# Where the down projection keeps its weight sums and its operand slots, and when its last stores are issued

## Chip, cores and metric

One NeuronCore of a Trainium2 chip runs the kernel. The metric is the device time of one execution in microseconds (us). Five engines work side by side, each on its own list of instructions in order: TensorE (PE, matrix products), VectorE (DVE), ScalarE (ACT), GpSimd (POOL) and SyncE (SP), whose list here holds the DMA issues. An engine that waits for a semaphore holds up everything behind it on its own list.

## What is computed

The model has two layers. Each is a mixer, then a feed-forward part (FFN), then a gated residual (PLE). The change lies in the second product of the FFN, `w_down`, and touches the seam to the PLE behind it:

```python
def swiglu(h, w_gate, w_up, w_down):
    return (jax.nn.silu(h @ w_gate) * (h @ w_up)) @ w_down
...
        h = h + swiglu(rmsnorm(h, norm_ffn_g[i]), ffn_w_gate[i], ffn_w_up[i], ffn_w_down[i])
        e = rmsnorm(p[i] @ ple_w_proj[i], ple_post_norm_g[i])
        h = h + e * jax.nn.sigmoid(rmsnorm(h, ple_norm_g[i]) @ ple_w_gate[i])
```

There are 1024 rows, 1024 columns in the model and 2816 in the FFN, all in fp32. A product of fp32 operands is made of three products of halves: each operand is split into a high half (a cast on ScalarE, line 108) and a low half (operand minus high half, on VectorE, line 109), and high by high, high by low and low by high are added up.

## The kernel before, in words

Gate/up and down both use a Winograd form of the 2 x 2 block product: seven block products instead of eight, each of sums of blocks. `wino` makes four such sums of four blocks, in four operations of 128 x 512. On GpSimd it makes the sums `S` of gate/up's weights (in a pool of two buffers), the sums `Sg` of each of the 11 pairs of gated activations `g`, and the sums `T_dn` of each of the 11 raw weights `wr_dn` of down.

Gate/up (`ffn_gu`) goes over the pairs j = 0 to 10, two groups (gate, up) for each. The products of a group are called by their operand: B11, T1, T2, B21 (bank pgc), T3, B22 (bank pgb, operand tiles HB22h and HB22l), T4. Lines 867, 869 and 871 add the banks into `g` or `u`; lines 935 to 937 multiply u into g. Seven blocks of each pair (three of g, four of Sg) are stored to DRAM in `gfD` (lines 940 to 942).

Down (`ffn_down`) reads these back. It works in four units of pairs: (0, 1), (2, 3, 4), (5, 6, 7), (8, 9, 10). A unit has seven steps, one for each block product. "Step 1.0" below is step 0 of unit 1. Step (gi, wi) uses the stored block gi and the weight block wi, where wi 0 to 3 are blocks of the raw weight and 4 to 7 are the sums T_dn. A step needs a slot of four parts: x (block as stored, later its low half), y (its high half), wh and wl (halves of the weight block). Its work is: a get of x on SP (line 1011), y on ScalarE (line 1016), x minus y on VectorE (line 1017), wh and wl of each pair of the unit (lines 108, 109), then on TensorE 4 x 3 x m matmuls for m pairs (line 1027; 24 in unit 0, 36 in the others), and an evacuation of four banks into `h` (a copy on ScalarE, or an addition on VectorE, line 1030). TensorE alternates two sets of four banks, pda and pdb. In unit 0 the four pdb banks of step 1 are banks that gate/up used.

Memory is divided by pools that are opened in an order written by hand, so that each tile comes to lie on memory that an earlier stage has done with. The kernel's framework makes the instruction wait that first writes there. The slots of down are one large tile `sl12` (six parts of 8 KB for each partition), the pools s0 and s7, `s3` and, once, the two buffers `hn`. T_dn_0 and T_dn_1 (pool `tc_`, two buffers) lie behind `sl12`, on the memory of HB22h and HB22l. The order of instructions on each engine comes from a scheduler that follows the program text and priorities; `self.after([...])` tells it not to place what is inside ahead of the named instruction. Unit 0's preparation is held that way behind `last_sum`, the last line 869.

`ple` follows. It splits the weights of its gate (wr_pg to wh_pg and wl_pg, lines 1118 and 1119, the latter on GpSimd), and norms the rows of h (ss_p on GpSimd, hn_p on VectorE line 203, transposes on line 193). Its first splits and norms are placed among the last steps of down.

Of the kernel before, what the change touches and what calls it, by code (L numbers as in the profile page):

```python
# [9 lines left out]
F32 = mybir.dt.float32  # L10
# [53 lines left out]
class _K:  # L64
# [712 lines left out]
    def wino(self, eng, dst, b, role):  # L777


        sub = lambda o, x, y: eng.tensor_tensor(o, x, y, op=ALU.subtract)  # L780
        if role == "left":
# [3 lines left out]
            sub(dst[3], b[1], dst[1])  # L785
        else:
# [3 lines left out]
            sub(dst[3], b[2], dst[1])  # L790

    def ffn(self, l):
# [3 lines left out]
        with ExitStack() as es:  # L796
# [21 lines left out]
            self.ffn_gu(sp, fp, {"Ta": ta_, "Tb": tb_}, l, H, gD, right)  # L818
# [3 lines left out]
        with ExitStack() as es:  # L822
            self.ffn_down(es, l, gD)
# [3 lines left out]
    def ffn_gu(self, sp, fp, tp_, l, H, gD, right):  # L827
# [98 lines left out]
        for j in range(NFF // 2):  # L926
# [12 lines left out]
            self.wino(gp, [S[:, i] for i in range(4)], [g[:, 0, 0], g[:, 1, 0], g[:, 0, 1], g[:, 1, 1]], "left")  # L939
            nc.sync.dma_start(gD[j, :, 0:2, :], g[:, :, 0, :])  # L940
            nc.sync.dma_start(gD[j, :, 2, :], g[:, 1, 1, :])
            nc.sync.dma_start(gD[j, :, 3:7, :], S)

    def ffn_down(self, es, l, gD):
# [9 lines left out]
        s12 = mk(3).tile([P, 6 * 2048], F32R, name=f"sl12_{l}")  # L954
        self.pad(es, 1, f"ffp2{l}")
        tc_ = mk(6)
        s7 = mk(7)
        self.pad(es, 2, f"ffp3{l}")
        s3 = mk(8)

        slots = itertools.chain((s0, 0, 2, None, 4, s0, 0), (s7, 3, s0, 0) * 3 + (s7, 3), (s0, 0, 3, s0, 0, 3, 0))
# [6 lines left out]
        units = ((0, 1), (2, 3, 4), (5, 6, 7), (8, 9, 10))  # L968
        seen = set()
# [10 lines left out]
        for ui, pairs in enumerate(units):  # L980
            m = len(pairs)
            ws = []
            for p in pairs:
# [4 lines left out]
                self.wino(gp, [T[:, i] for i in range(4)], [q[:, i] for i in range(4)], "right")  # L988
# [5 lines left out]
            for si, (gi, wi, chain, first, (hr, hc)) in enumerate(steps):  # L994
# [4 lines left out]
                slot = next(slots)  # L999
                if slot is None:  # L1000
                    x, y = [self.np.tile([P, D], F32R, tag="hn", bufs=2, name=f"sl{f}{nm}").rearrange("p (j n) -> p j n", j=2) for f in "xy"]
                    slot = s3.tile([P, 2, 2, 512], F32R, name=f"slw{nm}")
                    wh, wl = slot[:, 0], slot[:, 1]
                else:
                    if isinstance(slot, int):
                        slot = s12[:, slot * 2048:][:, :m * 2048]
                    else:
                        slot = slot.tile([P, 6144], F32R, tag="slot", bufs=1, name=f"sl{nm}")[:, :m * 2048]
                    slot = slot.rearrange("p (i j n) -> p i j n", i=4, j=m)
                    x, y, wh, wl = [slot[:, i] for i in range(4)]  # L1010
# [751 lines left out]
```

## Time and profile before

| what | us |
|---|---|
| time before, median of 3 runs | 2976.1 (2974.38 to 2976.13) |
| the profiled execution, its own time | 2976.15 |
| span of the profile of that execution | 2974.3 |
| TensorE busy | 2867.7 (96% of the span) |
| VectorE busy | 1867.2 (63%) |
| GpSimd busy | 1060.5 (36%) |
| granted TensorE clock, mean | 0.985 of full |
| down, layer 0 (first to last matmul) | 1130.5 to 1353.8 |
| down, layer 1 | 2650.0 to 2872.5 |

The profile is of one execution, and its times are counted from the start of the span. The time of an execution is 1.85 us longer than the span. A busy share is an average over stages; how a stage is bound is read from that stage's own rows: what TensorE waited for there, and what the engines that it waited for were doing.

### The profile page before, as it was taken

The numbers are of one execution on the slowest core, as the hardware profiler recorded it, in microseconds if no ns is written. First come the engines' busy times: TensorE is split into PE (matmuls) and PEld (weight loads), VectorE is DVE, ScalarE is ACT, GpSimd is POOL, SyncE is SP. The second block draws the span as 40 slices with busy tenths as digits, with TensorE's granted clock in tenths as the row PEclk, the third lists the DMA queues.
The fourth block names the chain that finished last, engine by engine and source line by source line (L and its number), as shares of the span: only waits on it lengthen the run. The fifth ranks groups of instructions, "written<-read, shape, count | busy, mean of one in ns | idle before, by whom it ended". The sixth has DMA issues, their size and how long they took to land.

```text
span 2974.3 us, 47842 instructions
## 1 busy us (share of the span) xinstructions
PE 2867.7 (96%) x19211; PEld 2388.5 (80%) x19211; DVE 1867.2 (63%) x3274; ACT 1259.4 (42%) x2226; POOL 1060.5 (36%) x931
## 2 busy tenths in 40 slices
PE   7999998999999998999999999999999999999999
PEld 6989876797888886888887777788678888878887
DVE  5799995455444448885466767664445444479871
ACT  4467725544333335434445455443233333344341
POOL 1341000114544436435212443342144455556333
PEclk9999998999999999999999999999999999999999
DMA  4122165201322225534332232223711322245422
GB/s 146 50 51 93 57 191 201 90 30 38 112 106 95 103 107 216 190 108 139 107 127 97 94 111 97 87 94 110 266 64 71 113 102 95 105 172 206 162 87 92
DMA packets 119822, 340.80 MB, mean 115 GB/s; under 512 B 11696, under 2 KB 34608, under 8 KB 101936
## 3 DMA queue, kind: packets, MB, share of 16 engines
q1 hardware_dynamic: 119600, 337.74, 32.9%
q8 instruction: 151, 2.47, 0.3%
q14 instruction: 71, 0.58, 0.1%
HBM read 240.64 MB, written 97.06 MB: 114 GB/s over the span
## 4 chain that ended last, share of the span: by engine, by line
PE 83%; DVE 8%; DMA 3%; ACT 3%; issue 2%; POOL 1%; SPq 0%; DVEq 0%; ACTq 0%; POOLq 0%
PE pga L852 16%; PE pgb L852 8%; PE pso L1369 7%; PE pdb L1027 6%; PE pda L1027 6%; PE psp L1138 6%; PE psz L216 4%; PE pgc L852 4%; PE pskqv L227 3%; PE psow L237 3%; PE psz L1629 2%; PE y L743 2%; PE pswob L237 2%; DVE sc L467 1%; PE tpp L734 1%
## 5 line engine op out<-in xcount | busy, mean ns | idle before, releaser
L1027 PE MATMUL pda<-sl 128*128 128x512 f32 x912 | 217.5, 396 | 12.4 <-DVE sl L109 12.3
L1027 PEld LDWEIGHTS pda<-sl 128*128 128x128 f32 x912 | 173.9, 191 | 51.7 <-DVE sl L109 15.4
L1027 PE MATMUL pdb<-sl 128*128 128x512 f32 x888 | 207.9, 391 | 5.4 <-DVE g L937 3.7
L782 POOL TENSOR_TENSOR S<-wr_gu 128x512 f32<-128x512 f32 x44 | 68.8, 1563 | 395.9 <-DMA wr_gu<-in_w_gu_dram 373.8
L1027 PEld LDWEIGHTS pdb<-sl 128*128 128x128 f32 x888 | 167.1, 189 | 41.9 <-DVE g L937 4.1
L109 DVE TENSOR_TENSOR w2l_gu<-S,w2h_gu 128x1024 fp32r<-128x1024 f32 x44 | 67.2, 1528 | 164.4 <-ACT w2h_gu L108 164.3
L1369 PE MATMUL pso<-hh,wl_od 128*128 128x512 f32 x384 | 157.3, 410 | 0.0
L1369 PE MATMUL pso<-hh,wh_od 128*128 128x512 f32 x384 | 156.9, 409 | 0.0
L1369 PE MATMUL pso<-hl,wh_od 128*128 128x512 f32 x384 | 156.4, 407 | 0.0
L1016 ACT CAST sl<-sl 128x1536 fp32r<-128x1536 f32 (+1 forms) x54 | 74.8, 1386 | 145.8 <-DMA sl<-gfD 143.1
L108 ACT CAST w2h_gu<-S 128x1024 fp32r<-128x1024 f32 x44 | 46.3, 1052 | 186.1 <-PE pga L852 94.1
L1387 DVE SCALAR_TENSOR_TENSOR c<-pso,odcw,c 128x509 f32<-128x509 f32 (+1 forms) x144 | 107.0, 743 | 26.5 <-ACT c L1384 24.9
L1017 DVE TENSOR_TENSOR sl<-sl 128x1536 fp32r<-128x1536 f32 (+1 forms) x54 | 103.3, 1914 | 24.7 <-ACT sl L1016 24.5
L227 PE MATMUL pskqv<-wh_kqv,hh 128*128 128x256 f32 x384 | 109.4, 285 | 0.3 <-ACT wh_kqv L108 0.3
L227 PE MATMUL pskqv<-wh_kqv,hl 128*128 128x256 f32 x384 | 108.7, 283 | 0.0
L227 PE MATMUL pskqv<-wl_kqv,hh 128*128 128x256 f32 x384 | 108.3, 283 | 0.0
L603 DVE TENSOR_SCALAR_CACHE_REDUCE tk_junk<-sc,tk_f 128x1024 int8<-128x1024 f32 (+5 forms) x111 | 102.5, 924 | 1.8
L153 POOL TENSOR_SCALAR nss_f<-nss_f 128x1 f32<-128x1 f32 x16 | 3.2, 200 | 273.2 <-ACT junk_f L152 273.2
L1138 PE MATMUL psp<-wh_pg,hh_p 128*128 128x512 f32 x256 | 100.5, 393 | 0.0
L1138 PE MATMUL psp<-wh_pg,hl_p 128*128 128x512 f32 x256 | 99.7, 390 | 0.0
L1138 PE MATMUL psp<-wl_pg,hh_p 128*128 128x512 f32 x256 | 99.7, 389 | 0.0
L600 ACT ACTIVATE tk_junka<-sc,tk_f 128x512 int8<-128x512 f32 (+2 forms) x93 | 83.7, 900 | 34.5 <-DVE tk_f L618 30.3
(543 smaller groups left out, 9013.3 us busy)
## 6 DMA issues: line engine op xcount, KB each, us to landing
wr_gu<-in_w_gu_dram SPq DMA_DIRECT2D x44, 1024.0 KB
sl<-gfD SPq DMA_DIRECT2D x42, 768.0 KB
gfD<-Sg SPq DMA_DIRECT2D x22, 1024.0 KB
wr_dn<-in_w_dn_dram SPq DMA_DIRECT2D x22, 1024.0 KB
wr_od<-in_w_qkv_dram SPq DMA_DIRECT2D x12, 1024.0 KB
cD<-c SPq DMA_DIRECT2D x24, 512.0 KB
gfD<-g SPq DMA_DIRECT2D x22, 512.0 KB
wr_z<-in_w_z_dram SPq DMA_DIRECT2D x10, 1024.0 KB
```

The costliest lines, as they stand in the source:

```text
L216: nc.tensor.matmul(ps[:M, f * 512:(f + 1) * 512], a[:, kc, c], b[f][:, kc, :], start=(kc == 0 and i == 0), stop=(kc == KC - 1 and i == 2))
L227: nc.tensor.matmul(out, a[:, kc, c], b[:, kc, :], start=(kc == 0 and i == 0), stop=(kc == KC - 1 and i == 2))
L237: nc.tensor.matmul(ps[:, f * 512:(f + 1) * 512], a[:, kc, tsl], b[:, f * 512:(f + 1) * 512], start=(kc == 0 and i == 0), stop=(kc == nk - ...
L600: nc.scalar.activation(jk[:, :n], sc[b], AF.Sign, bias=fb, scale=-1.0, accum_out=c)
L603: v.tensor_scalar(jk[:, :n], sc[b], fb, 0.0, op0=op, op1=ALU.add, accum_out=c)
L852: nc.tensor.matmul(bank, a[:, kc, :], b[:, kc, :], start=first and kc == 0 and m == 0, stop=kc == 3 and m == 2, skip_group_check=True)
L1016: nc.scalar.copy(y, x.bitcast(F32))
L1017: v.tensor_tensor(x, x.bitcast(F32), y.bitcast(F32), op=ALU.subtract)
L1027: nc.tensor.matmul(ps, a[:, i, c], b[:, i, :], start=first and i == 0 and k == 0, stop=i == m - 1 and k == 2, skip_group_check=True)
L1138: nc.tensor.matmul(ps, a[:, kc, c], b, start=kc == 0 and i == 0, stop=kc == KC - 1 and i == 2)
L1369: nc.tensor.matmul(ps[:, f * 512:(f + 1) * 512], a[:, kc, :], b[f][:, kc, :], start=(kc == 0 and i == 0), stop=(kc == KC - 1 and i == 2))
L1387: nc.vector.scalar_tensor_tensor(c[:, e:(f + 1) * 512], ps[:, e - d:(f + 1) * 512 - d], cw[:, k:k + 1], c[:, e:(f + 1) * 512], op0=ALU.mul ...
```

## The change

The down stage is re-divided. The four points that touch the order of work are these.

- `sl12` is replaced by `sa` (32 KB), `sb` (16 KB) and a smaller `s3`. The pool of T_dn_0 and T_dn_1 now comes right behind `sa`, which is the memory of gate/up's weight sums S_20 and S_21; `sb` now lies on HB22h and HB22l.
- `slots` is written anew. Unit 0: n0, a, the middle of `sa`, own (the `hn` buffers and `s3`), sb, n0, a. Units 1 and 2 go round c, n7, n0, a, where c is made of parts of `sb`, `sa` and `s3`. Unit 3: n0, a, c, n0, a, n0, a. A slot is thus used again three steps on at step 1.0, and two steps on at steps 3.5 and 3.6.
- The last pair's three stores are issued behind the get of step 0.6. The sums of unit 1's weights are placed behind the Sg sums of the last pair.
- A step's preparation from unit 1 on is placed behind the preparation of the step before and the evacuation of the third step before.

In `ple` the pool w0 is split in two, so that the first high half lies elsewhere than the other three.

```diff
@@ wino
-        sub = lambda o, x, y: eng.tensor_tensor(o, x, y, op=ALU.subtract)
+        sub = lambda o, x, y: eng.tensor_tensor(o, x, y, op=ALU.subtract).ins
...
-            sub(dst[3], b[1], dst[1])
+            return sub(dst[3], b[1], dst[1])
...
@@ ffn_gu
-            self.wino(gp, [S[:, i] for i in range(4)], [g[:, 0, 0], g[:, 1, 0], g[:, 0, 1], g[:, 1, 1]], "left")
-            nc.sync.dma_start(gD[j, :, 0:2, :], g[:, :, 0, :])
-            nc.sync.dma_start(gD[j, :, 2, :], g[:, 1, 1, :])
-            nc.sync.dma_start(gD[j, :, 3:7, :], S)
+            self.last_Sg = self.wino(gp, [S[:, i] for i in range(4)], [g[:, 0, 0], g[:, 1, 0], g[:, 0, 1], g[:, 1, 1]], "left")
+
+            def store(j=j, g=g, S=S):
+                nc.sync.dma_start(gD[j, :, 0:2, :], g[:, :, 0, :])
+                nc.sync.dma_start(gD[j, :, 2, :], g[:, 1, 1, :])
+                nc.sync.dma_start(gD[j, :, 3:7, :], S)
+
+            if j < NFF // 2 - 1:
+                store()
+        return store
@@ ffn_down
-        s12 = mk(3).tile([P, 6 * 2048], F32R, name=f"sl12_{l}")
+        piece = lambda i, kb: mk(i).tile([P, kb * 256], F32R, name=f"sl{i}_{l}")
+        sa = piece(3, 32)
         self.pad(es, 1, f"ffp2{l}")
         tc_ = mk(6)
+        sb = piece(4, 16)
         s7 = mk(7)
         self.pad(es, 2, f"ffp3{l}")
-        s3 = mk(8)
-
-        slots = itertools.chain((s0, 0, 2, None, 4, s0, 0), (s7, 3, s0, 0) * 3 + (s7, 3), (s0, 0, 3, s0, 0, 3, 0))
+        s3 = piece(8, 8)
+
+        cut = lambda *at: lambda n, nm: [t[:, a if b is None else b * n:][:, :n] for t, a, b in at]
+        run = lambda t, a=0: lambda n, nm: [t[:, a + i * n:a + (i + 1) * n] for i in range(4)]
+        new = lambda p: lambda n, nm: run(p.tile([P, 6144], F32R, tag="slot", bufs=1, name=f"sl{nm}"))(n, nm)
+
+        def own(n, nm):
+            return [self.np.tile([P, D], F32R, tag="hn", bufs=2, name=f"sl{f}{nm}") for f in "xy"] + [s3[:, :n], s3[:, n:2 * n]]
+
+        n0, n7, a, c = new(s0), new(s7), run(sa), cut((sb, 0, 0), (sb, 0, 1), (sa, 6144, None), (s3, 0, 0))
+        slots = itertools.chain((n0, a, run(sa, 4096), own, run(sb), n0, a), (c, n7, n0, a) * 3 + (c, n7), (n0, a, c, n0, a, n0, a))
...
-                self.wino(gp, [T[:, i] for i in range(4)], [q[:, i] for i in range(4)], "right")
+                with self.after([self.last_Sg] if ui == 1 else None):
+                    self.wino(gp, [T[:, i] for i in range(4)], [q[:, i] for i in range(4)], "right")
...
-                nc.sync.dma_start(x.bitcast(F32), gD[pairs[0]:pairs[-1] + 1, :, gi, :].rearrange("j p n -> p j n"))
+                x, y, wh, wl = [t.rearrange("p (j n) -> p j n", j=m) for t in next(slots)(m * 512, nm)]
+                get = nc.sync.dma_start(x.bitcast(F32), gD[pairs[0]:pairs[-1] + 1, :, gi, :].rearrange("j p n -> p j n")).ins
+                if (ui, si) == (0, 6):
+                    with self.after([get]):
+                        store()
...
-                with self.after([self.last_sum] if ui == 0 and si else None):
+                with self.after(prep + evac[:1] if ui else [self.last_sum] if si else None):
                     nc.scalar.copy(y, x.bitcast(F32))
                     v.tensor_tensor(x, x.bitcast(F32), y.bitcast(F32), op=ALU.subtract)
                     for i in range(m):
-                        self.split(wh[:, i], wl[:, i], ws[i][wi])
+                        prep = list(self.split(wh[:, i], wl[:, i], ws[i][wi]))
...
+                evac = evac[-2:] + [out.ins]
@@ ple
-            self.pad(es, 17, f"plp0{l}")
-            w0 = mk("w0")
+            self.pad(es, 1, f"plp0{l}")
+            w0 = [mk("w0a")]
+            self.pad(es, 16, f"plp1{l}")
+            w0 += [mk("w0b")] * 3
...
-                    wt = [(w1[kh] if u else w0).tile([P, 4, 512], F32R, name=f"w{f}_pg{l}_{u}{kh}") for f in "hl"]
+                    wt = [(w1[kh] if u else w0[2 * kh + i]).tile([P, 4, 512], F32R, name=f"w{f}_pg{l}_{u}{kh}") for i, f in enumerate("hl")]
```

The lists of instructions show what this does to the order. TensorE's order in down is the same. On GpSimd, layer 0, behind the Sg sums of pair 9, there stood before:

```order
L780 TENSOR_TENSOR T_dn0_0_9476<-wr_dn0_0_9472 128x512 x2
L780 TENSOR_TENSOR T_dn0_1_9481<-wr_dn0_1_9474 128x512 x2
L780 TENSOR_TENSOR T_dn0_0_9476<-wr_dn0_0_9472,T_dn0_0_9476 128x512
L780 TENSOR_TENSOR T_dn0_1_9481<-wr_dn0_1_9474,T_dn0_1_9481 128x512
L780 TENSOR_TENSOR T_dn0_0_9476<-wr_dn0_0_9472,T_dn0_0_9476 128x512
L780 TENSOR_TENSOR T_dn0_2_9750<-wr_dn0_2_9604 128x512 x2
L780 TENSOR_TENSOR T_dn0_1_9481<-wr_dn0_1_9474,T_dn0_1_9481 128x512
L780 TENSOR_TENSOR T_dn0_2_9750<-wr_dn0_2_9604,T_dn0_2_9750 128x512
L780 TENSOR_TENSOR T_dn0_3_9755<-wr_dn0_3_9606 128x512 x2
L782 TENSOR_TENSOR Sg0_10_9409<-g0_10_9177 128x512
L780 TENSOR_TENSOR Sg0_10_9409<-g0_10_9177 128x512
```

and now there stands, up to the first sums of unit 1:

```order
L780 TENSOR_TENSOR T_dn0_0_9478<-wr_dn0_0_9474 128x512 x2
L780 TENSOR_TENSOR T_dn0_0_9478<-wr_dn0_0_9474,T_dn0_0_9478 128x512 x2
L780 TENSOR_TENSOR T_dn0_1_9483<-wr_dn0_1_9476 128x512 x2
L780 TENSOR_TENSOR T_dn0_1_9483<-wr_dn0_1_9476,T_dn0_1_9483 128x512 x2
L782 TENSOR_TENSOR Sg0_10_9409<-g0_10_9177 128x512
L780 TENSOR_TENSOR Sg0_10_9409<-g0_10_9177 128x512
L780 TENSOR_TENSOR Sg0_10_9409<-Sg0_10_9409,g0_10_9177 128x512
L780 TENSOR_TENSOR Sg0_10_9409<-g0_10_9177,Sg0_10_9409 128x512
L780 TENSOR_TENSOR T_dn0_2_9754<-wr_dn0_2_9605 128x512 x2
L780 TENSOR_TENSOR T_dn0_3_9759<-wr_dn0_3_9607 128x512 x2
```

The eight sums of each kind are no longer mixed: first T_dn0_0, then T_dn0_1, then the Sg sums of the last pair, then the sums of unit 1's weights.

On VectorE, layer 1, from the last line 869 on (sl1_0_0 is the slot of step 0, slx and slw or sl8 belong to step 3, the remaining sl are the slots of steps 1, 2 and 4; lines 1017 and 1027 are the same operation before and after), before:

```order
L869 TENSOR_TENSOR u1_10_24401<-pga1_21_24421,u1_10_24401 128x512
L109 TENSOR_TENSOR sl12_1_24562<-wr_dn1_0_24580,sl12_1_24562 128x512
L1017 TENSOR_TENSOR slx1_0_3_24708<-slx1_0_3_24708,sly1_0_3_24709 128x1024
L1017 TENSOR_TENSOR sl12_1_24562<-sl12_1_24562 128x1024
L936 TENSOR_TENSOR g1_10_24285<-u1_10_24401,g1_10_24285 128x512
L871 TENSOR_TENSOR u1_10_24401<-pgb1_21_24422,u1_10_24401 128x512
L109 TENSOR_TENSOR sl1_0_0_24598<-wr_dn1_1_24582,sl1_0_0_24598 128x512
L109 TENSOR_TENSOR sl12_1_24562<-wr_dn1_1_24582,sl12_1_24562 128x512
L109 TENSOR_TENSOR slw1_0_3_24710<-T_dn1_0_24584,slw1_0_3_24710 128x512
L937 TENSOR_TENSOR g1_10_24285<-pga1_21_24421,g1_10_24285 128x512
```

and now:

```order
L869 TENSOR_TENSOR u1_10_24416<-pga1_21_24436,u1_10_24416 128x512
L109 TENSOR_TENSOR sl3_1_24574<-wr_dn1_0_24597,sl3_1_24574 128x512
L1027 TENSOR_TENSOR slx1_0_3_24725<-slx1_0_3_24725,sly1_0_3_24726 128x1024
L109 TENSOR_TENSOR sl8_1_24596<-T_dn1_0_24601,sl8_1_24596 128x512
L1027 TENSOR_TENSOR sl3_1_24574<-sl3_1_24574 128x1024
L936 TENSOR_TENSOR g1_10_24300<-u1_10_24416,g1_10_24300 128x512
L109 TENSOR_TENSOR sl3_1_24574<-T_dn1_0_24601,sl3_1_24574 128x512
L871 TENSOR_TENSOR u1_10_24416<-pgb1_21_24437,u1_10_24416 128x512
L109 TENSOR_TENSOR sl4_1_24585<-T_dn1_0_24601,sl4_1_24585 128x512
L109 TENSOR_TENSOR sl1_0_0_24615<-wr_dn1_1_24599,sl1_0_0_24615 128x512
L109 TENSOR_TENSOR sl3_1_24574<-wr_dn1_1_24599,sl3_1_24574 128x512
```

The low half that step 0 still lacks, sl1_0_0 from wr_dn1_1, came right behind line 871, and now comes behind three low halves of T_dn1_0 more, one of them ahead of line 936 and one on either side of line 871.

On SP, layer 0, from the last pair's first store (line 941, 940 and 942 before; 942, 943 and 944 after) to the gets of unit 1 (lines 1011 and 1018 are the same operation), before:

```order
L941 DMA gfD0_6508<-g0_10_9177 128x512
L940 DMA gfD0_6508<-g0_10_9177 128x2x512
L1011 DMA sl0_0_5_9679<-gfD0_6508 128x2x512
L976 DMA wr_dn0_5_9926<-in_w_dn0_dram 128x2048
L976 DMA wr_dn0_6_9928<-in_w_dn0_dram 128x2048
L1011 DMA sl12_0_9454<-gfD0_6508 128x2x512
L942 DMA gfD0_6508<-Sg0_10_9409 128x2048
L1011 DMA sl12_0_9454<-gfD0_6508 128x3x512
L1011 DMA sl0_1_0_9765<-gfD0_6508 128x3x512
```

and now, from the get of step 0.5 on:

```order
L1018 DMA sl0_0_5_9680<-gfD0_6508 128x2x512
L993 DMA wr_dn0_5_9930<-in_w_dn0_dram 128x2048
L993 DMA wr_dn0_6_9932<-in_w_dn0_dram 128x2048
L1018 DMA sl3_0_9451<-gfD0_6508 128x2x512
L942 DMA gfD0_6508<-g0_10_9177 128x2x512
L943 DMA gfD0_6508<-g0_10_9177 128x512
L944 DMA gfD0_6508<-Sg0_10_9409 128x2048
L1048 DMA hres0_0_9926<-hB_67 128x1024
L1018 DMA sl0_1_1_9822<-gfD0_6508 128x3x512
L1048 DMA hres0_1_10037<-hB_67 128x1024
L1018 DMA sl4_0_9462<-gfD0_6508 128x3x512
```

The stores of g moved behind the get of step 0.6, the get of step 1.1 (sl0_1_1) follows the store of Sg and one hres, and the get of step 1.0 (sl4, three blocks) comes last.

## Rows read from the trace of the kernel before

**Rows 1.** The page: the span, and the costliest group (busy, mean ns, idle before).

```profile
span 2974.3 us, 47842 instructions
...
L1027 PE MATMUL pda<-sl 128*128 128x512 f32 x912 | 217.5, 396 | 12.4 <-DVE sl L109 12.3
```

**Rows 2.** Timeline, TensorE, layer 0 (start, us, engine line op, out<-in, count [idle<-releaser]).

```profile
1127.64 0.50 PE L852 MATMUL pga<-HT4h,w2h_gu 128*128 128x512 f32 x1 [0.32 <-DVE u L869]
...
1130.50 5.63 PE L1027 MATMUL pda<-sl 128*128 128x512 f32 x24
...
1143.89 2.93 PE L1027 MATMUL pdb<-sl 128*128 128x512 f32 x6 [3.68 <-DVE g L937]
...
1152.18 7.54 PE L1027 MATMUL pda<-sl 128*128 128x512 f32 x23 [4.94 <-DVE sl L109]
...
1176.07 5.60 PE L1027 MATMUL pda<-sl 128*128 128x512 f32 x24
1181.51 8.32 PE L1027 MATMUL pdb<-sl 128*128 128x512 f32 x36
```

**Rows 3.** Timeline, TensorE, the first unit of layer 1.

```profile
2650.03 1.09 PE L1027 MATMUL pda<-sl 128*128 128x512 f32 x4
2652.19 4.81 PE L1027 MATMUL pda<-sl 128*128 128x512 f32 x20 [1.06 <-DVE sl L109]
...
2669.00 8.53 PE L1027 MATMUL pda<-sl 128*128 128x512 f32 x23 [6.33 <-DVE sl L109]
...
2699.95 8.59 PE L1027 MATMUL pdb<-sl 128*128 128x512 f32 x36 [0.48 <-DVE h L1030]
```

**Rows 4.** Windows, layer 0: us; busy of PE, PEld, DVE, ACT, POOL; clock; DMA.

```profile
1130.50:1181.50 51.00, 42.34 (x169) 33.35 (x168) 47.54 (x39) 23.80 (x39) 48.00 (x26) 0.87 0.60 218
1181.50:1353.80 172.30, 171.67 (x758) 141.82 (x757) 145.62 (x164) 66.63 (x85) 69.53 (x38) 1.00 0.43 150
```

**Rows 5.** Timeline, GpSimd, both layers, around the first sums of down.

```profile
1097.30 1.30 POOL L780 TENSOR_TENSOR Sg<-g,Sg 128x512 f32<-128x512 f32 x1 [0.45 <-DVE g L937]
1127.40 6.92 POOL L780 TENSOR_TENSOR T_dn<-wr_dn 128x512 f32<-128x512 f32 x4 [28.80 <-PE pgb L852]
...
2647.51 7.47 POOL L780 TENSOR_TENSOR T_dn<-wr_dn 128x512 f32<-128x512 f32 x4 [26.01 <-PE pgb L852]
```

**Rows 6.** Timeline, VectorE, layer 0, around the end of gate/up.

```profile
1123.85 0.69 DVE L109 TENSOR_TENSOR sl<-wr_dn,sl 128x512 fp32r<-128x512 f32 x1 [1.29 <-ACT sl L108]
1125.63 1.23 DVE L1017 TENSOR_TENSOR sl<-sl 128x1024 fp32r<-128x1024 f32 x1 [1.09 <-ACT sl L1016]
...
1127.50 3.44 DVE L109 TENSOR_TENSOR sl<-wr_dn,sl 128x512 fp32r<-128x512 f32 x2
1130.86 2.31 DVE L1017 TENSOR_TENSOR slx<-slx,sly 128x1024 fp32r<-128x1024 f32 x1
...
1143.15 0.68 DVE L937 TENSOR_TENSOR g<-pga,g 128x512 f32<-128x512 f32 x1
```

**Rows 7.** Timeline, VectorE and ScalarE, layer 1, around the end of gate/up.

```profile
2645.17 0.69 DVE L869 TENSOR_TENSOR u<-pga,u 128x512 f32<-128x512 f32 x1 [2.42 <-PE pga L852]
...
2648.37 1.14 ACT L108 CAST sl<-wr_dn 128x512 fp32r<-128x512 f32 x2 [1.58 <-DMA wr_dn<-in_w_dn_dram]
```

**Rows 8.** Timeline, VectorE, ScalarE and TensorE, steps 3.3 to 3.6 of layer 0.

```profile
1326.21 1.76 DVE L1017 TENSOR_TENSOR sl<-sl 128x1536 fp32r<-128x1536 f32 x1 [1.01 <-ACT sl L1016]
...
1336.55 8.32 PE L1027 MATMUL pda<-sl 128*128 128x512 f32 x36
...
1342.16 1.46 ACT L1016 CAST sl<-sl 128x1536 fp32r<-128x1536 f32 x1
...
1343.66 3.59 DVE L1017 TENSOR_TENSOR sl<-sl 128x1536 fp32r<-128x1536 f32 x1
...
1347.31 6.64 PE L1027 MATMUL pdb<-sl 128*128 128x512 f32 x28 [0.63 <-DVE sl L1017]
```

**Rows 9.** Timeline, SyncE's queue, layer 0, behind the last Sg store.

```profile
1164.52 4.89 SPq L1011 DMA_DIRECT2D sl<-gfD  x2
```

## What I predict, and how

> **What bounds the kernel now.** I read the page first: TensorE is the engine that ends the program, and among its costliest groups only the product of the down stage (line 1027) shows idle time ahead of it worth naming, most of it released by VectorE's low halves on line 109 [rows 1]. The change touches only this stage and its two seams, so I next read TensorE's rows in order of time there. In layer 0 the first unit of down (7 steps of 24 matmuls) runs from 1130.50 to 1181.51, 51.0 us [rows 2]. A step at full speed is 5.44 us (1176.07 to 1181.51), or 0.2267 a matmul, so the unit could take 38.1: 12.9 us are lost. Of these 3.68 are a wait for line 937 in step 1 and 4.94 a wait for line 109 in step 2; most of the rest is slow matmuls behind the waits: 23 of them take 7.54 us from 1152.18 instead of 22 x 0.2267 and 0.39 for the last, 5.38, so 2.16 more. In layer 1 the unit takes 2650.03 to 2699.95, 49.9 us [rows 3]: 11.8 lost, with waits of 1.06, 6.33 and 0.48, and 3.15 of slow matmuls behind the 6.33. The granted clock falls to 0.87 in layer 0's first unit and is 1.00 in the three units behind it, where TensorE is busy 171.67 of 172.30 us [rows 4]. So some 24.7 us in all lie in two places, and each other unit runs at the bound.
>
> Why VectorE is late there: GpSimd stands still for 28.80 and 26.01 us, then starts the sums of the first unit's weights when the last pgb product of gate/up has been issued [rows 5], because these sums were placed in the memory of an operand of that product. From then on both engines are busy for nearly the whole unit, 47.54 and 48.00 of 51.0 us [rows 4], and every VectorE operation with two inputs in SBUF is slower: a low half of 512 columns takes 0.69 alone and 1.72 beside GpSimd (3.44 for two), the 1024-column difference 1.23 and 2.31 [rows 6]. GpSimd's own operation takes 1.30 alone and 1.73 so (6.92 for four) [rows 5].
>
> **The change, part by part.** (1) *Sums earlier.* Their memory is now that of gate/up's weight sums. In layer 0 the first weight has been there for long, and GpSimd is idle from 1098.6 (the last Sg operation begins at 1097.30 [rows 5]); the second is there at about 1123.2, where ScalarE reads it and VectorE's first low half of it follows at 1123.85 [rows 6]. So eight sums at 1.3 to 1.73 end at about 1130 instead of running on past 1144. The four of the second weight now lie beside the drain of gate/up: the low half at 1123.85 ends at 1125.6, the difference at 1125.63 takes 2.31 instead of 1.23, and line 869, which releases the last T4 product, moves by 1.08. T4 waited 0.32 for it at 1127.64 [rows 2] and has no cover: **+1.0**. Behind it GpSimd has nothing to do until line 935 has run, so VectorE goes at its own price: from 1128.5 two low halves, still partly contended (2.8), one clean (0.7), two differences (1.2 each), a low half, line 871, a low half, line 936, three low halves, a difference: some 12 us, line 937 begins at about 1140.2. Step 1, now starting at 1136.9, needs it 18 matmuls later at 1141.0 and step 2 needs its operands at 1142.4. Both waits and their slow matmuls go: **-12.9**, with almost no slack at line 937 (a late half microsecond costs a half).
>
> (2) *Layer 1: a wait moves forward.* There step 0's second low half no longer stands right behind line 871 but three low halves and two differences later. Its weight lands at 2648.37 [rows 7], GpSimd's four sums of it start with it and take 6.9 us, to 2655.3. VectorE: line 869 ends at 2645.86 [rows 7]; a clean low half, difference, low half bring it to 2648.5. Then a difference at 2.31, line 936 and a low half at 1.72 each, line 871 at 0.68, a low half, the last part of it clean (1.0), and the awaited one at 0.7: about 2656.6. TensorE stops for it at 2651.13, where the 1.06 wait began [rows 3]. The wait is 5.5 us; all clean it would be 2.0, all contended 7.2. Behind 4.94 the slow matmuls cost 2.16 and behind 6.33 3.15, so 2.5 here. Then nothing else is late: GpSimd is again idle while VectorE makes steps 1 and 2, ready by about 2661, needed at 2663.5 and 2668.9. Cost 8.0 instead of 11.8: **-3.8** (from 0 when all is contended to -9.7 when clean).
>
> (3) *Slots.* Step 1.0 (unit 1, step 0) takes the slot of step 0.4, so its get may go out only when step 0.4 has ended, two steps (10.9 us) ahead; before, it had a free slot. The nearest row is the slot of step 3.6, also used two steps before: free at 1336.55, its cast on ScalarE at 1342.16 to 1343.62, its difference 1.76 clean or 3.59 contended [rows 8], so ready 8.9 to 10.7 us after. Needed after 10.88 and two matmuls: slack 0.6 to 2.4. On SP the get stands behind that of step 1.1, which now waits for the store of the last Sg to land; a 1 MB store held the queue 4.9 us [rows 9]. With line 935 at about 1143 the Sg sums end at 1150, the store lands at 1155, ahead of 1158.7, where step 0.4 ends; were it all in the way, the stall would be 10.7 + 4.9 - 11.3 = 4.3. Bounds 0 and 4.3; I take **+1.0** a layer, nearer to the quiet row. (4) *Step 3.5* is now at distance two as well, and wl_pg is cut into an early and a late part. In step 3.6 the 3.59 of the difference beside wl_pg cost 0.63 [rows 8]; with half of wl_pg gone this goes, and step 3.5 may take some of it: **-0.3** a layer, bounds -0.6 and +0.6. (5) The last pair's stores go out later; only unit 3 reads them, 60 us on: 0. TensorE's order and all counts are unchanged.
>
> Sum: layer 0: -12.9 + 1.0 + 1.0 - 0.3 = -11.2; layer 1: -3.8 + 1.0 - 0.3 = -3.1; together -14.3. The profiled execution took 2976.15 (span 2974.3 and 1.85 around it), the median is 2976.1: **2961.8**.
>
> The contended 1.72 is less than the two engines' times in turn (0.69 + 1.30). The Trainium skill (SBUF — State Buffer, "Who interferes with whom") has such an operation of VectorE and one of GpSimd that reads SBUF shut each other out for the whole instruction, which speaks against laying the sums beside the drain. By it each contended operation would be 1.99: T4 some 0.3 and layer 1's awaited half some 1.1 later, a sum of -12.9 instead of -14.3. I stay with the row.
>
> **Rivals.** *Both layers without a wait*: layer 1's half comes at its clean bound, a wait of 2.0 with no slow matmuls (as behind the 1.06), and unit 1 finds its slot: -11.9 - 9.8 - 0.6 = -22.3, 2953.9. For it: VectorE's clean times; against it: GpSimd has the second weight at the same moment. *Unit 1 starts late*: the get of step 1.0 meets the store and a contended difference: 4.3 and 1.4 of slow matmuls (as behind the 3.68: six take 2.93 instead of 1.52 [rows 2]) in place of 1.0, a layer: -14.3 + 9.4 = -4.9, 2971.2; half of it 2966.5. For it the slack of 0.6; against it SP's room of 3.7 us. *The change doesn't do what it says*: only the first weight's sums come early, the second's are held by its late landing and push line 937 and step 2 back by the 3.7 and 4.9 us, halved: -14.3 + 6.5 = -7.8, 2968. *Slower*: the new order hints tie VectorE's preparation to two or three steps ahead, so it can't work ahead for a run of GpSimd sums. A step of three pairs costs it 3.59 + 3 x 1.72 + 4 x 0.68 = 11.5 contended against 8.16 of TensorE: 3.3 lost a step. The twelve sums for units 2 and 3 last some 19 us each time, 2.3 steps: 7.7 a unit, 31 for four units: 2993. It ends on the slower side if more than about six of these nine contended steps show it (20 us). Against it: in these units VectorE is busy 145.62 of 172.30 and GpSimd 69.53 [rows 4], 6.9 a step, and step 1.0's stall would itself give room.
>
> **How the numbers follow.** Forecast 0.52, no wait 0.15, late unit 1 0.17, not as said 0.07, slower 0.09. The range takes in the forecast with its bounds, the first rival and most of the second: 2950 to 2972. About 0.2% (6 us) is what a measurement of this kernel can tell from no change: faster (under 2970.1) holds the forecast, the first rival and two thirds of the second and third, 0.80; same 0.11; slower 0.09.
>
> **What would show it.** Right: GpSimd's first T_dn sums before 1112 and idle from 1130 to line 935; no wait in steps 1 and 2 of layer 0; T4's wait 1.3; in layer 1 one wait of 4 to 7 us about 1 us into step 0 for line 109, none of 6 in step 2. Wrong: a wait at the first matmuls of unit 1 over 2 us, waits for line 109 or 1027 of the new kernel within units 1 to 3, or sums that start at the pgb's end as before.

## The result, and the profile after

The changed kernel takes 2957.28 us (median of 4 runs, 2953.6 to 2959.56); in the same runs the kernel before takes 2976.11 (2974.38 to 2978.62). The ratio is 0.9935, its interval 0.9918 to 0.9952. Predicted were 2961.8 and a range of 2950 to 2972. The profiled execution is the quickest of the four, with a span of 2951.7 against 2974.3.

The page after, the rows that answer to [rows 1] (the product of down is now line 1037):

```profile
span 2951.7 us, 47874 instructions
...
L1037 PE MATMUL pda<-sl 128*128 128x512 f32 x912 | 214.4, 393 | 5.0 <-DVE sl L109 5.0
```

Of 12.4 us of idle time ahead of the group 5.0 are left, and they are one wait.

The stage is measured here from down's first matmul to the first transposes of the stage behind it (tp_p), and unit 0 to the first matmul of unit 1:

| us | before | after | difference |
|---|---|---|---|
| unit 0, layer 0 | 51.01 | 38.31 | -12.70 |
| units 1 to 3, layer 0 | 172.28 | 171.91 | -0.37 |
| unit 0, layer 1 | 49.92 | 46.26 | -3.66 |
| units 1 to 3, layer 1 | 172.55 | 171.36 | -1.19 |

Down has thus lost 13.07 and 4.85, and T4's longer wait gives 0.52 back: -17.4. The spans differ by 22.6. The other 5.2 lie outside down: 3.6 ahead of it in layer 0 and 1.6 between the two layers' down; behind layer 1's down both profiles take 101.8. A second profile of the changed kernel (after_again, below) shows that as much lies between two executions of one kernel: its layer 0 reaches down at 1131.64 instead of 1127.42. The medians differ by 18.8.

TensorE's timeline after, layer 0 (start, us, engine line operation, out<-in, count, idle before and its releaser), which answers to [rows 2]:

```profile
1124.55 0.50 PE L852 MATMUL pga<-HT4h,w2h_gu 128*128 128x512 f32 x1 [0.84 <-DVE u L869]
...
1127.42 5.65 PE L1037 MATMUL pda<-sl 128*128 128x512 f32 x24
...
1165.73 0.61 PE L1037 MATMUL pdb<-sl,sl 128*128 128x512 f32 x2
1166.60 8.01 PE L1037 MATMUL pdb<-sl,sl 128*128 128x512 f32 x34 [0.25 <-DVE sl L1027]
```

The seven steps of unit 0 follow each other without a wait, at 5.43 to 5.59 each. T4 waits 0.84, and the third matmul of unit 1 waits 0.25. The same view of layer 1, which answers to [rows 3]:

```profile
2632.26 1.10 PE L1037 MATMUL pda<-sl 128*128 128x512 f32 x4
2638.35 7.50 PE L1037 MATMUL pda<-sl 128*128 128x512 f32 x20 [4.99 <-DVE sl L109]
```

The waits of 1.06 and 6.33 have become one of 4.99, ahead of the fifth matmul of step 0. The 20 matmuls behind it take 7.50, where 19 x 0.2267 + 0.39 = 4.70 would do. The windows view of unit 0 of either layer (columns as in [rows 4]) shows what this does to the engines:

```profile
1127.40:1165.70 38.30, 38.30 (x169) 31.55 (x168) 32.02 (x35) 19.59 (x31) 27.18 (x18) 1.00 0.80 295
2632.30:2678.50 46.20, 41.21 (x169) 33.35 (x168) 35.51 (x36) 22.52 (x34) 37.15 (x24) 0.93 0.71 254
```

In layer 0 TensorE is busy all the time at a granted clock of 1.00 (0.87 before), and GpSimd's 48.00 us of work in the unit have become 27.18. Where the rest went stands in GpSimd's timeline, layer 0 and then layer 1:

```profile
1102.65 2.55 POOL L780 TENSOR_TENSOR T_dn<-wr_dn 128x512 f32<-128x512 f32 x2 [7.65 <-DMA wr_dn<-in_w_dn_dram]
...
1119.80 3.01 POOL L780 TENSOR_TENSOR T_dn<-wr_dn 128x512 f32<-128x512 f32 x2 [11.99 <-DMA wr_dn<-in_w_dn_dram]
1122.78 3.95 POOL L780 TENSOR_TENSOR T_dn<-wr_dn,T_dn 128x512 f32<-128x512 f32 x2
1138.45 1.69 POOL L782 TENSOR_TENSOR Sg<-g 128x512 f32<-128x512 f32 x1 [11.72 <-DVE g L935]
...
2630.90 3.49 POOL L780 TENSOR_TENSOR T_dn<-wr_dn 128x512 f32<-128x512 f32 x2 [17.85 <-DMA wr_dn<-in_w_dn_dram]
```

In layer 0 all eight sums are done by 1126.7, ahead of down; GpSimd then stands 11.72 us until line 935, and VectorE has the memory to itself. In layer 1 the second weight lands only at about 2630.8, so its sums lie beside the start of down.

### The profile page after: what moved, and what is told of

The parts are those of the page before. It is cut to its first block, busy times and chain, and to the rows that moved or that the text cites. A ratio compares the mean times of both kernels' runs of the same rounds, so it can differ in the third digit from the quotient of the medians.

```text
span 2951.7 us, 47874 instructions
## 1 busy us (share of the span) xinstructions
PE 2857.1 (97%) x19211; PEld 2382.9 (81%) x19211; DVE 1860.2 (63%) x3274; ACT 1256.3 (43%) x2226; POOL 1054.1 (36%) x931
## 4 chain that ended last, share of the span: by engine, by line
PE 81%; DVE 9%; ACT 3%; DMA 3%; issue 2%; POOL 1%; SPq 0%; DVEq 0%; ACTq 0%; POOLq 0%
PE pga L852 16%; PE pgb L852 8%; PE pso L1382 7%; PE pdb L1037 7%; PE pda L1037 6%; PE psp L1151 6%; PE psz L216 4%; PE pgc L852 4%; PE psow L237 3%; PE psz L1642 2%; PE pskqv L227 2%; PE y L743 2%; PE pswob L237 2%; DVE sc L467 1%; PE tpp L734 1%
## 5 line engine op out<-in xcount | busy, mean ns | idle before, releaser
L1037 PE MATMUL pdb<-sl 128*128 128x512 f32 x528 | 122.3, 389 | 0.0
L1037 PEld LDWEIGHTS pdb<-sl 128*128 128x128 f32 x528 | 99.1, 188 | 20.6
```

Source lines behind the costliest of these rows:

```text
L1037: nc.tensor.matmul(ps, a[:, i, c], b[:, i, :], start=first and i == 0 and k == 0, stop=i == m - 1 and k == 2, skip_group_check=True)
```

## The experiments

The diffs are against the changed kernel, or, where a kernel builds on another experiment, against that one. Times of down are from the profile of each run, layer 0 and layer 1; the changed kernel's are 210.22 and 217.62 (and 209.68 and 215.45 in after_again), the kernel before has 223.29 and 222.47.

**Is it the early sums?** Their start is held back to where it was.

```diff
+                if p == 0:
+                    hold = [gp.memset(sb[:, 0:1].bitcast(F32), 0.0).ins]
-                with self.after([self.last_Sg] if ui == 1 else None):
+                with self.after([self.last_Sg] if ui == 1 else None if ui else hold):
```

> The changed kernel, but GpSimd writes one column of sb (the memory of HB22, free when the last pgb product has read it) ahead of the first unit's eight sums, so that these start as late as they did before the change; slots, stores and the other order stay new. Theory (the time of the sums decides): in layer 0 the waits of 3 to 5 us in steps 1 and 2 come back and unit 0 takes 47 to 52 us instead of 38.3; in layer 1 unit 0 takes 47 to 51 instead of 46.3, with its long wait at step 2 again; T4's wait is back to about 0.3. Rival (the new slots and order made the gain): unit 0 stays at 38 to 40 in layer 0.

Measured: 2975.86 us (one run), down 220.76 and 220.21. TensorE's timeline in the first units, line 1039 being the product of down:

```profile
1144.62 1.65 PE L1039 MATMUL pdb<-sl 128*128 128x512 f32 x6 [1.57 <-DVE g L937]
1151.92 7.37 PE L1039 MATMUL pda<-sl 128*128 128x512 f32 x23 [5.42 <-DVE sl L109]
...
2670.80 7.39 PE L1039 MATMUL pda<-sl 128*128 128x512 f32 x23 [6.29 <-DVE sl L109]
```

The waits for lines 937 and 109 are back at the places of [rows 2, 3], with 1.57 for 3.68, 5.42 for 4.94 and 6.29 for 6.33, and T4's wait is back at 0.32. All of the gain but some 2.5 us a layer hangs on when the sums run. That makes the early sums necessary; whether they are enough is for the next two.

**Do the new hints matter?** The prediction had the new order hints of units 1 to 3 at no gain, and as the source of its slower rival.

```diff
-                with self.after(prep + evac[:1] if ui else [self.last_sum] if si else None):
+                with self.after([self.last_sum] if ui == 0 and si else None):
```

> The changed kernel with the old hint: preparation from unit 1 on isn't tied to the step before and to the third evacuation before. VectorE then makes low halves further ahead, between the evacuations. Theory (the hints only tidy; VectorE has 15% to spare in units 1 to 3): from the first matmul of unit 1 to the first transposes of the next stage 171.5 to 172.3 us a layer, as with them (171.9 and 171.4), and unit 0 as with them. Rival of the prediction (the hints take away VectorE's lead and cost time): without them 0.3 to 2 us less a layer, no wait at unit 1. Other rival (the slots, used again two or three steps on, need them): waits of 1 us or more within units 1 to 3.

Measured: 2977.55 us (one run), down 221.74 and 222.58: nearly the whole gain is gone, with the sums as early as in the changed kernel. TensorE's and ScalarE's timelines, layer 0:

```profile
1164.69 2.93 PE L1037 MATMUL pda<-sl 128*128 128x512 f32 x6 [5.99 <-ACT h L1042]
1175.68 5.74 PE L1037 MATMUL pda<-sl 128*128 128x512 f32 x24 [2.27 <-DVE h L1040]
...
1162.59 0.62 ACT L108 CAST sl<-T_dn 128x512 fp32r<-128x512 f32 x1 [13.29 <-POOL T_dn L780]
1164.06 0.58 ACT L1042 COPY h<-pda 128x512 f32<-128x512 f32 x1
```

Without the hint a cast of unit 1's weight sums stands ahead of unit 0's evacuations on ScalarE. It waits 13.29 us for GpSimd, the evacuation behind it (line 1042) comes late, and TensorE finds no free PSUM bank for 5.99 and, a little later, 2.27 us. Layer 1 loses 5.0: beside the old 4.99 there is a wait of 2.50 for an evacuation that stands behind low halves on VectorE, and one of 1.50 at unit 1. The theory had no change here, and the prediction's rival a gain. The hints keep preparation out of the evacuations' way, and the changed kernel, which has them, waits only 0.25 in units 1 to 3.

**Do the later stores matter?** The last pair's stores are issued at once.

```diff
-            if j < NFF // 2 - 1:
-                store()
+            store()
...
-                if (ui, si) == (0, 6):
-                    with self.after([get]):
-                        store()
```

> The changed kernel with the last pair's three stores issued as soon as their data is there, so ahead of the gets of steps 0.5 and 0.6 on SP. Theory (the place of these stores costs nothing either way): SP waits for the last Sg sum until about 1146 on the scale of the changed kernel's profile, the get of step 0.5 then lands by 1151, needed at 1155; unit 0 of layer 0 stays at 38.1 to 38.7 us, no wait over 0.3. Rival (with unit 0 13 us shorter the stores are in the way): a wait of 1 to 4 us in step 5 or 6 of unit 0, or at unit 1.

Measured: 2966.7 us (one run), down 216.65 and 217.25: 6.4 more in layer 0, nothing in layer 1. The prediction and the theory had no effect at all. The timelines of SyncE's queue, ScalarE and TensorE, layer 0:

```profile
1148.46 0.32 SPq L944 DMA_DIRECT2D gfD<-Sg  x1
1148.88 0.38 SPq L1017 DMA_DIRECT2D sl<-gfD  x1
...
1154.74 1.04 ACT L1022 CAST sl<-sl 128x1024 fp32r<-128x1024 f32 x1 [16.04 <-DMA sl<-gfD]
1156.73 1.55 ACT L1038 COPY h<-pda 128x512 f32<-128x512 f32 x3
...
1157.36 8.59 PE L1033 MATMUL pda<-sl 128*128 128x512 f32 x24 [3.85 <-ACT h L1038]
```

The store of Sg waits on SP until its sums are done, and the get of step 0.5 waits behind it until 1148.88; in the changed kernel that get goes out at 1133.10. Its cast holds ScalarE for 16.04 us, with step 2's evacuations behind it. Nobody reads the stored data for over 100 us (unit 3's first get goes out at 1266.62), but what is queued behind the store is needed at once.

**The split of w0.** The pool is made whole again.

```diff
-            self.pad(es, 1, f"plp0{l}")
-            w0 = [mk("w0a")]
-            self.pad(es, 16, f"plp1{l}")
-            w0 += [mk("w0b")] * 3
+            self.pad(es, 17, f"plp0{l}")
+            w0 = [mk("w0")] * 4
```

> The changed kernel with the pool of the next stage's first weight halves whole again, so that all four operations of line wl_pg stand together on GpSimd near step 3.6. Theory (the 0.63 wait in step 3.6 came from VectorE's difference beside these four): the difference there takes 3.2 to 3.6 us again instead of 1.8, and a wait of 0.4 to 0.8 us in step 3.5 or 3.6 is back in both layers. Rival (the new slots and hints removed it): no wait, and the same time as the changed kernel.

Measured: 2961.15 us (one run), down 209.68 and 217.53, no wait at step 3.5 or 3.6. Its GpSimd and VectorE timelines:

```profile
1309.74 9.48 POOL L1130 TENSOR_TENSOR wl_pg<-wr_pg,wh_pg 128x1024 fp32r<-128x1024 f32 x4 [13.15 <-ACT wh_pg L1129]
...
1331.01 1.76 DVE L1027 TENSOR_TENSOR sl<-sl 128x1536 fp32r<-128x1536 f32 x1 [0.39 <-ACT sl L1026]
```

wl_pg runs in one piece, 21 us ahead of the difference of step 3.6 and not beside it. The 0.63 of [rows 8] is gone either way, so the split isn't needed for that; the theory fails. Why wl_pg comes so early here was not looked into.

**What makes layer 1's wait?** First a kernel without the second weight's four sums (weight 1 uses those of weight 0).

```diff
+                if p == 1:
+                    T = T0
+                else:
-                with self.after([self.last_Sg] if ui == 1 else None):
-                    self.wino(gp, ...)
+                    with self.after([self.last_Sg] if ui == 1 else None):
+                        self.wino(gp, ...)
+                T0 = T
```

> The changed kernel without the four sums of the second weight (steps that use them read those of the first weight, so GpSimd does nothing beside the end of gate/up and the begin of down). Theory (layer 1's wait is made by the row's place and by VectorE's slower operations beside these sums): the wait of 5.0 us in step 0 of layer 1 falls to 1 to 2 us, its slow matmuls from 2.8 to under 0.4, unit 0 there takes 39.3 to 40.7 instead of 46.3; in layer 0 T4's wait falls from 0.8 to about 0.3. Rival (the place in VectorE's list alone decides): the wait in layer 1 stays above 4 us.

Measured: 2954.79 us (one run), down 209.68 and 214.66. The wait is shorter but stands (TensorE, then VectorE ahead of it, layer 1):

```profile
2638.95 6.46 PE L1041 MATMUL pda<-sl 128*128 128x512 f32 x20 [3.08 <-DVE sl L109]
...
2637.01 1.28 DVE L109 TENSOR_TENSOR sl<-T_dn,sl 128x512 fp32r<-128x512 f32 x2
2638.21 1.29 DVE L109 TENSOR_TENSOR sl<-wr_dn,sl 128x512 fp32r<-128x512 f32 x2
```

Every low half now takes 0.69, so GpSimd no longer slows VectorE, and still TensorE waits 3.08: from line 869 on, six low halves of T_dn stand ahead of the awaited half, where the changed kernel has three (its rows are in the next section). This run alone therefore doesn't split the wait cleanly; it shows that order has a part in it. So the order was changed next: step 0's halves ahead of the others of unit 0.

```diff
-                    for i in range(m):
-                        prep = list(self.split(wh[:, i], wl[:, i], ws[i][wi]))
+                    with self.after(p0 if ui == 0 and si > 1 else None):
+                        for i in range(m):
+                            prep = list(self.split(wh[:, i], wl[:, i], ws[i][wi]))
+                if ui == 0 and si == 0:
+                    p0 = prep[1:]
```

> The changed kernel with the low halves of steps 2 to 6 of unit 0 placed behind step 0's last low half; in layer 1 this half then comes right behind line 871, as before the change, and GpSimd's sums stay where they are. Theory (place and contention): it is ready about 1.5 us after TensorE stops, so the wait falls from 5.0 to 1 to 2 us and the slow matmuls behind it from 2.8 to under 0.4; unit 0 of layer 1 takes 39.5 to 41 instead of 46.3, the whole some 6 us less than the changed kernel. Rival (the wait moves on to step 1 or 2, since the halves moved back are then late): unit 0 of layer 1 still takes 44 or more, with a new wait for line 109 or 1027.

Measured: 2956.22 us (0.9927, 0.991 to 0.9943), down 209.66 and 215.82, which is within what two profiles of the changed kernel differ by. TensorE and VectorE, layer 1:

```profile
2634.26 5.89 PE L1040 MATMUL pda<-sl 128*128 128x512 f32 x24
2645.71 1.07 PE L1040 MATMUL pda<-sl 128*128 128x512 f32 x4
2650.11 6.44 PE L1040 MATMUL pda<-sl 128*128 128x512 f32 x20 [3.33 <-DVE sl L109]
...
2644.39 1.77 DVE L109 TENSOR_TENSOR sl<-T_dn,sl 128x512 fp32r<-128x512 f32 x1
...
2648.30 1.75 DVE L109 TENSOR_TENSOR sl<-T_dn,sl 128x512 fp32r<-128x512 f32 x1
```

Step 0 runs through, and the wait now stands at the same place of step 2, whose second half comes last on VectorE, behind the Sg sums that have begun meanwhile (1.77 and 1.75 instead of 0.69). T4's wait stayed: 0.92. The next kernel also puts step 0's difference of layer 0 behind the last line 869.

```diff
+                    with self.after([self.last_sum] if l == ui == si == 0 else None):
-                    v.tensor_tensor(x, x.bitcast(F32), y.bitcast(F32), op=ALU.subtract)
+                        v.tensor_tensor(x, x.bitcast(F32), y.bitcast(F32), op=ALU.subtract)
```

> As half_first, and in layer 0 the difference of step 0 is placed behind line 869, which releases T4. Theory (that difference, slowed by GpSimd, is what T4 waited 0.8 us for): T4 waits under 0.2, step 0 starts on time, and layer 0 gains 0.6 to 0.8 us more. Rival (step 0's operand now comes late in its place): a wait of 0.5 us or more at the first matmuls of down in layer 0, no gain.

Measured: 2955.71 us (0.9922, 0.9907 to 0.9937), down 209.76 and 216.57. The T4 row of layer 0 and the wait of layer 1:

```profile
1124.41 0.50 PE L852 MATMUL pga<-HT4h,w2h_gu 128*128 128x512 f32 x1 [0.32 <-DVE u L869]
...
2648.72 7.60 PE L1041 MATMUL pda<-sl 128*128 128x512 f32 x20 [3.33 <-DVE sl L109]
```

T4 is back at 0.32: that difference was its whole loss, 0.5 us. In the medians neither kernel can be told from the changed one. To get step 2's half earlier, VectorE must be kept from preparing later steps ahead of it. Three ways were tried; all build on half_first_sum. The first puts the preparation of steps 3 and 4 (counted from 0) behind that of the step before:

```diff
-                with self.after(prep + evac[:1] if ui else [self.last_sum] if si else None):
+                with self.after(prep + evac[:1] if ui else [self.last_sum] + (prep if si in (3, 4) else []) if si else None):
```

> As half_first_sum, and in unit 0 the preparation of step 3 is placed behind that of step 2 and that of step 4 behind that of step 3, so that step 2's last low half no longer stands behind line 935's successors and step 4's difference. In half_first_sum that half, beside the Sg sums, made a wait of 3.33 us and 3.1 us of slow matmuls in step 2 of layer 1. Theory (the row's place beside GpSimd's work): it is ready at about 2642.5, before step 2 begins at 2643.5, and the wait goes; unit 0 of layer 1 takes 38.3 to 40 instead of 46.3 in the changed kernel, layer 0 stays at 38.1 to 38.6; the whole some 6 to 8 us less than the changed kernel. Rival (what is moved back is late in its turn): a new wait of 1 to 4 us at step 3 or 4 of unit 0, and unit 0 of layer 1 above 42.

Measured: 2967.69 us (0.996, 0.9941 to 0.998), down 214.55 and 221.68, worse than the changed kernel by 4 in either layer. Layer 1, VectorE and TensorE:

```profile
2662.88 3.41 DVE L109 TENSOR_TENSOR sl<-T_dn,sl 128x512 fp32r<-128x512 f32 x2
...
2667.88 0.68 DVE L1044 TENSOR_TENSOR h<-pdb,h 128x512 f32<-128x512 f32 x1
...
2668.61 1.22 PE L1041 MATMUL pdb<-sl,sly 128*128 128x512 f32 x2 [7.38 <-DVE h L1044]
```

Preparation at contended prices now stands ahead of an evacuation, and TensorE waits 7.38 us for the PSUM bank. In layer 0 the loss lies at unit 1, with waits of 0.80 and 1.87 (its gets are in the next section). The second way holds only step 4, behind step 2's halves:

```diff
-                if ui == 0 and si == 0:
-                    p0 = prep[1:]
+                if ui == 0:
+                    p0, p2 = (prep[1:], None) if si == 0 else (p0, prep[1:] if si == 2 else p2)
...
-                with self.after(prep + evac[:1] if ui else [self.last_sum] if si else None):
+                with self.after(prep + evac[:1] if ui else [self.last_sum] + (p2 if si == 4 else []) if si else None):
```

> As half_first_sum, with step 4's preparation behind that of step 2 only, so still ahead of step 1's evacuations. Theory: the 3.33 wait in step 2 goes, but step 1's first evacuation now stands behind step 4's contended difference and halves and comes at about 20 us after down's first matmul, so step 3 waits 1.5 to 4 us for it (its bank); unit 0 of layer 1 41 to 45 us. Rival (the evacuations have slack there): no wait over 0.5, under 40 us.

Measured: 2956.16 us (one run), down 209.76 and 218.02. Step 2's wait has gone, and the bank wait stands in its place, shorter; unit 1 now waits 0.92 and 1.06 besides, and down as a whole is no shorter than in half_first_sum:

```profile
2652.02 0.73 PE L1041 MATMUL pdb<-sl,sly 128*128 128x512 f32 x2 [2.47 <-DVE h L1044]
```

The third puts step 4's preparation behind that evacuation too. It was timed on one chip beside the changed kernel itself (after_again).

```diff
-    [self.last_sum] + (p2 if si == 4 else [])
+    [self.last_sum] + (p2 + evac[:1] if si == 4 else [])
```

> The changed kernel as it is, timed beside the version below on one chip. Theory: 0.992 to 0.995 of the kernel before; in its trace unit 0 of layer 0 takes 38.1 to 38.7 us, of layer 1 46 to 47, as in its first profile, and any other difference between its executions lies outside down.

> As half_first_sum, and the preparation of step 4 of unit 0 is placed behind that of step 2 and behind the evacuation of step 1, as the changed kernel does it from unit 1 on. Theory (VectorE's list in layer 1's first 20 us is what binds: step 2's last half, then step 1's evacuations, then step 4): no wait in step 2, no wait for an evacuation, and one of 0 to 2 us at step 4 for line 109; unit 0 of layer 1 39 to 41.5 us instead of 46.3, layer 0 at 38.1 to 38.7; the whole 4 to 7 us less than the changed kernel on the same chip. Rival (this much work beside GpSimd can't be made in time in any order): unit 0 of layer 1 stays at 43 or more, the whole within 2 us of half_first_sum.

Measured: after_again 2956.76 us (0.9926, 0.9913 to 0.994), half_evac 2951.72 (0.9907, 0.9892 to 0.9921). Down is 209.68 and 215.45 against 209.65 and 212.29. TensorE in layer 1, after_again and then half_evac:

```profile
2641.62 6.41 PE L1037 MATMUL pda<-sl 128*128 128x512 f32 x20 [3.92 <-DVE sl L109]
```

```profile
2640.13 4.83 PE L1041 MATMUL pda<-sl 128*128 128x512 f32 x20 [1.07 <-DVE sl L109]
...
2679.20 8.00 PE L1041 MATMUL pdb<-sl,sl 128*128 128x512 f32 x34 [0.97 <-DVE sl L1028]
```

Unit 0 of layer 1 takes 39.66 instead of 44.09 (1.6 over its bound of 38.1), though a wait of 0.97 comes back at unit 1. With T4's 0.5 the trace shows 3.7 us; the medians differ by 5.0, with intervals that just overlap. It is the quickest of all kernels here.

## Why the prediction was right, point by point

**Layer 0, unit 0: -12.9 predicted, -12.70 measured.** Line 937 runs at 1135.41, 8.0 us after down's first matmul, where the working had 8.7 (1140.2, with down put off by T4 to 1131.5); both waits and all slow matmuls are gone. The mechanism, GpSimd's sums out of VectorE's way, is confirmed by late_sums. The working had a gap all the same: it priced the new hints and the later stores at nothing, and without the one or the other 11.5 or 6.4 us of layer 0 are lost (old_hints, store_now). Both are cover for the gain: a late step on ScalarE's or SP's queue there isn't hidden, since evacuations or gets stand behind it.

**T4: +1.0 predicted, +0.52 measured.** VectorE's timeline after, layer 0, beside [rows 6]:

```profile
1120.35 1.30 DVE L109 TENSOR_TENSOR sl<-wr_dn,sl 128x512 fp32r<-128x512 f32 x1 [1.40 <-ACT sl L108]
1122.13 1.76 DVE L1027 TENSOR_TENSOR sl<-sl 128x1024 fp32r<-128x1024 f32 x1 [0.48 <-ACT sl L1026]
```

The difference took 1.76 and not 2.31, although GpSimd works all through it (1119.80 to 1126.73, above). What was priced wrongly is how much of a sum it meets: it began 0.68 us ahead of the end of GpSimd's second sum (1122.81) and ended 1.08 behind that end, while the 2.31 of [rows 6] began 1.23 ahead and ended 1.08 behind as well (the last section has the count). The 0.53 over the quiet 1.23 is what T4 lost, as half_first_sum shows. The Trainium skill (SBUF — State Buffer, "Who interferes with whom") has the two shut each other out for the whole instruction, 1.99 for a low half by the estimate ahead. The trace agrees that they take turns (by the ends counted in the last section), but low halves that met nearly a whole sum took 1.72 to 1.79, so for the price the row stands.

**Layer 1, unit 0: -3.8 predicted, -3.66 measured.** The wait is where it was expected. VectorE after, layer 1:

```profile
2631.48 1.79 DVE L936 TENSOR_TENSOR g<-u,g 128x512 f32<-128x512 f32 x1
2633.19 1.75 DVE L109 TENSOR_TENSOR sl<-T_dn,sl 128x512 fp32r<-128x512 f32 x1
2634.87 0.68 DVE L871 TENSOR_TENSOR u<-pgb,u 128x512 f32<-128x512 f32 x1
2635.47 1.15 DVE L109 TENSOR_TENSOR sl<-T_dn,sl 128x512 fp32r<-128x512 f32 x1
2636.55 2.35 DVE L109 TENSOR_TENSOR sl<-wr_dn,sl 128x512 fp32r<-128x512 f32 x2
```

Line 936 and a low half take 1.79 and 1.75 beside the sums, and the awaited half is the first of the last two. 4.99 and 2.80 of slow matmuls (predicted 5.5 and 2.5) replace 1.06, 6.33, 3.15 and 0.48. The second profile has 3.92 and 1.71, and the unit takes 44.09, 5.83 less than before: there line 936 begins just ahead of the sums and takes 0.68. The size thus hangs on when the last weight lands, and is good to some 2 us only; that -3.66 lies so near the -3.8 is luck.

**Unit 1's slot: +1.0 a layer predicted, 0.25 and 0 measured.** SyncE's queue after, layer 0:

```profile
1145.89 0.33 SPq L944 DMA_DIRECT2D gfD<-Sg  x1
...
1154.53 0.37 SPq L1018 DMA_DIRECT2D sl<-gfD  x1
...
1155.52 5.34 SPq L1018 DMA_DIRECT2D sl<-gfD  x2
```

The get at 1154.53 is step 1.1's, and it waits for the store to land, 8.6 us here and not the 4.9 of [rows 9]. Step 0.4's last matmul ends at 1155.0, and the get of step 1.0 goes out at 1155.52. So SP had a room of 0.5 us and not the 3.7 of the working. The cast of step 1.0 runs at 1162.59, and its difference from 1164.23 to 1166.55, 2.32 and not the 3.59 of the bound. That the later store and the cheaper difference nearly cancel is luck. The rival with a late unit 1 was near: in half_chain_sum the get of step 1.1 goes out at 1161.59, 0.5 us behind step 0.4's last matmul, and there unit 1 waits 0.80 and 1.87.

**Steps 3.5 and 3.6: -0.3 a layer predicted; the wait of 0.63 is gone.** GpSimd's and VectorE's rows after, layer 0:

```profile
1323.22 5.36 POOL L1132 TENSOR_TENSOR wl_pg<-wr_pg,wh_pg 128x1024 fp32r<-128x1024 f32 x2 [25.60 <-ACT wh_pg L1131]
...
1328.04 2.15 DVE L1027 TENSOR_TENSOR sl<-sl 128x1536 fp32r<-128x1536 f32 x1 [0.55 <-ACT sl L1026]
```

The late part of wl_pg begins 6.3 us ahead of step 3.6 (1329.48), as all of it did before the change (1338.45 for 1344.71), but is two operations instead of four. The difference meets only its end and takes 2.15 instead of the 3.59 of [rows 8], which is the reason that the prediction gave. By w0_whole the split is not the only way to it. Units 1 to 3 as a whole gained 0.37 and 1.19, where these two points had them lose 0.7 a layer. That makes 3.0 us and T4 0.5; less 0.3 in the two units 0, it is the 3.1 by which -17.4 lies below the -14.3.

**The slower rival** had the hints' sign reversed. Units 1 to 3 show no wait but the 0.25, and the kernel without the hints is the slow one. (Of the chances, the shares named for "faster" add up to 0.83 and not to 0.80.) The rival without waits needed layer 1's half clean; half_evac comes near to its unit, by order and not by a clean VectorE.

## What to carry to other kernels

Price every hint and every moved issue by what stands behind the instruction on its in-order queue: a cast or a store that waits for data costs nothing itself, and here cost 11.5 and 6.4 us of layer 0 by the evacuations and gets behind it. When an early sum frees an engine, look which preparation that engine does next and whether the next needed operand comes last in it; half_evac got 3.7 us by its trace, and 5.0 by the medians, by order alone. An operation of VectorE moved beside GpSimd's is to be priced by what is left of GpSimd's operation when it begins, not by the fully contended row.

## What the runs showed of the hardware

VectorE's low halves and differences take turns with GpSimd's operations; line 871, which reads a PSUM bank, keeps its 0.68 beside the sums. Over the 13 profiles here, 705 low halves of down's slots (128x512) began while an operation of GpSimd had 0.15 us or more still to run. Of these 688 ended 0.52 to 0.58 us behind the end of that operation; the other 17 took 0.67 to 0.69, as alone, and GpSimd's operation took longer (1.83 to 2.96). For the difference of 1024 columns it is 1.08 behind that end, in 76 of 77.

The get that waits on SP for the last pair's store of 1 MB went out 4.9 us behind that store before the change (1164.10 to 1169.04, [rows 9]) and 8.6 after it.

The slow matmuls behind a wait don't go by the length of that wait. After the same 3.33 us, the 20 matmuls behind took 6.44 in half_first and 7.60 in half_first_sum; windows of just these stretches show it in the granted clock (the last but two of the columns), half_first and then half_first_sum:

```profile
2650.11:2656.55 6.44, 6.44 (x21) 5.24 (x22) 6.44 (x7) 2.52 (x6) 6.44 (x4) 0.74 0.58 192
```

```profile
2648.72:2656.32 7.60, 7.60 (x21) 6.09 (x22) 7.60 (x9) 2.53 (x5) 7.60 (x5) 0.61 0.66 227
```

A mean clock of 0.74 or 0.61 means that a part of the stretch ran at the lower level of 1.2 GHz; behind it the clock is 1.00 again. Over the kernels shown, of this and of before, the extra time was 1.71 to 2.16 behind six waits for line 109 (3.08, 3.33, 3.92, 4.94, 5.42 and 6.29), and 2.80 to 3.15 behind three (3.33, 4.99, 6.33); behind those of 1.06 and 1.07 it was 0.1 to 0.2. Layer 1's wait of 5.00 cost 1.6 more in store_now and 2.7 more in w0_whole. What chooses between the two was not found out, so a wait of 3 to 6 us is to be priced at its length and 1.6 to 3.2 more.
